# Attention scores of a hybrid decoder layer: both products of a score block over all 128 rows of the array

## The chip, the core and the metric

The kernel runs on one core of a Trainium2 chip. A core has a matrix engine (TensorE, in the profile PE for its matmuls and PEld for its weight loads), a vector engine (VectorE, DVE), a scalar engine (ScalarE, ACT), a general engine (GpSimd, POOL) and a queue that mostly issues transfers (SyncE, SP). Each works through its own list of instructions in order, and they wait for each other by semaphores. TensorE multiplies a stationary operand, which is loaded into its array of 128 by 128 cells first, with a moving operand that streams past it. The rows of the array are the dimension over which is summed; an operand that lies on only 64 of the 128 partitions of the on-chip memory uses only 64 rows. Products are added up in PSUM.

The metric is the device time of one execution in microseconds (us).

## What is computed

One hybrid decoder layer on 512 tokens of width 1024, in float32: a layer norm, a token mixer made of an SSD (state space) branch and an attention branch, and a SwiGLU feed-forward part, each added to its input and normalized again. Only the attention branch is touched by the change. It has 16 query heads of width 64, two key heads (eight query heads share one), blocks of 128 queries, and a window of 128 keys:

```
qb = (q * (hd ** -0.5)).reshape(bsz, nb, ATT_BLOCK, nkv, ng, hd)
...
k_band = jnp.concatenate([kb[:, :-1], kb[:, 1:]], axis=2)
v_band = jnp.concatenate([vb[:, :-1], vb[:, 1:]], axis=2)
scores = jnp.einsum('bnqkgd,bnskd->bnkgqs', qb, k_band).astype(jnp.float32)
...
scores = jnp.where(valid[None, :, None, None], scores + bias, -jnp.inf)
...
m = jnp.maximum(jnp.max(scores, axis=-1, keepdims=True), sink)
p = jnp.exp(scores - m)
p = p / (jnp.sum(p, axis=-1, keepdims=True) + jnp.exp(sink - m))
out = jnp.einsum('bnkgqs,bnskd->bnqkgd', p.astype(v.dtype), v_band)
```

## The kernel before

All large products run in a float32 form of reduced width that TensorE takes quickly (fp32r). To keep the precision, each operand is split into a high part and a rest, `hi` and `lo`, and a product is made of three matmuls, hi times hi, hi times lo and lo times hi (`mm3`, lines 146 to 150). The weights come in 164 units of 128 by 1024 numbers. ScalarE makes the `hi` of a unit (line 134) and VectorE the `lo` (line 135), up to three units ahead of their use.

TensorE's order is written out by hand. The input layer norm and the first products (key, value, first query tile, and dt for the SSD decays) come first, up to about 49 us. Then the attention runs in eight steps t of two heads each. Between its parts a `Filler` emits pieces of other products (k-tile steps of three matmuls on `ps_mm`: the next query tiles, the first SSD group's inputs, the attention's gate), in fixed amounts `F_ATT`, so that TensorE has work while the softmax of a step is made on other engines. After the attention come the rest of the gate and the attention's output projection, the SSD, the mixing product and the feed-forward part.

One round of that loop (lines 652 to 671) emits on TensorE: the scores of step t+1 for its first head (8 matmuls), filler, the scores for its second head (8 matmuls), filler, the transposes of the probabilities of step t (`ps_pt`, line 477) with a little filler between the heads, the largest piece of filler, and the products with the values (`ps_o`, line 490, 16 matmuls), filler again. The other three engines' orders are made by a scheduler from the same program.

`scores(t)` (line 412) makes, for each head j and each half of the four query blocks, a PSUM tile `ps_sc` with two blocks n. A query tile `q_f` (`q`) holds for head j the query's `hi` on the head's own 64 partitions and the query's `lo` on the other 64 (`evac_q`, lines 390 to 398). A key tile `kd` holds the key's `hi` in column block 0 and its `lo` in column block 1, each of them on both halves of the partitions (`evac_k`, lines 625 to 629). So the first matmul of a block (line 432) runs over 128 rows and gives (hi + lo) of the query times hi of the key; the second (line 434) takes only the 64 partitions of `js`, and adds the query's hi times the key's lo. VectorE then puts the window together (line 439, `copy_predicated`) and adds the distance penalty (line 441). From there the softmax goes on: the maximum (line 447), exponentials on ScalarE (line 459), the sum and its reciprocal (lines 461 and 462), the scaling on GpSimd (line 464). The transposed probabilities are taken out of PSUM by ScalarE (line 479), GpSimd (line 480) and VectorE (line 483) into `pT`.

The eight matmuls of one head in one step follow each other without anything between them. They are called a score stretch below; there are 16 of them, and each is followed by filler.

Of the kernel before, what the change touches and what calls it, by code (L numbers as in the profile page):

```python
# [18 lines left out]
P = 128  # L19
S = 512  # L20
D = 1024
NT = S // P            # token tiles = chunks = query blocks
KD = D // P            # k-tiles of the model width
NQ = 8                 # q feature tiles (two heads each)
NG = 4                 # SSD groups
NH = 32                # SSD heads
NF = 22                # FFN hidden tiles
# [3 lines left out]
LAST = 7               # k-tiles of the last product that finish one token tile after the other  # L31
RAW = 4                # weight units loaded ahead
# amounts of products (0.65 for a k-tile step) between the parts of the attention and SSD chains
# [4 lines left out]
# order of the weight units in the packed array; each unit is [128, 1024]  # L38
U_K, U_V, U_Q = 0, 1, 2
U_XBC = 10             # 24 tiles: xs 16, B 4, C 4  # L40
# [4 lines left out]
U_YA = 74              # per group 4 units of [4 k-tiles x 256 columns]  # L45
U_MIX = 90             # per k-tile
U_FG = 98
U_FU = 120
U_FD = 142             # per k-tile
N_UNITS = 164  # L50

# columns of the packed per-partition parameters
C_CW = 0               # 24 x 4
C_CB = 96              # 24
C_DS = 120             # 16
C_NW = 136             # 16
C_DTB = 152            # 1
C_LN = 153             # 3 layer norms x (gain 8, bias 8)
# [4 lines left out]
def kernel(  # L63
# [15 lines left out]
    PSUM = bass.MemoryType.PSUM  # L79
# [8 lines left out]
    # ---------------------------------------------------------------- constants  # L88
# [19 lines left out]
    # ---------------------------------------------------------------- weights  # L108
    class Units:
        """Loads and splits the weight units in the order of their use."""  # L110
# [27 lines left out]

        def next(self, unit, kt=KD, ahead=None):
            """hi, lo of the unit as [128, kt, 1024 / kt]."""  # L140
            assert self.order[self.pos] == unit, (self.pos, self.order[self.pos], unit)
            self.prepare(self.pos + (self.ahead if ahead is None else ahead))
            self.pos += 1
            return tuple(a.rearrange("p (k n) -> p k n", k=kt) for a in self.split.pop(self.pos - 1))
# [7 lines left out]
    class Filler:  # L152
        """Products in steps of one k-tile, emitted between the parts of the attention and SSD chains."""
# [30 lines left out]
    # ---------------------------------------------------------------- layer norm  # L184
    def ln_stats(pl, src, between=None, cuts=(0, 512, 1024)):
        """Mean and sqrt(var + eps) of each row of src [128, 1024]."""
        n = len(cuts) - 1
        st = pl.tile([P, 4, 6], F32, name="ln_st", tag="ln_st", bufs=2)[:, 0:n]
        for i in range(n):
            nc.vector.bn_stats(out=st[:, i], in_=src[:, cuts[i]:cuts[i + 1]])  # L190
            if i == 0 and between:
                between()
        mv = pl.tile([P, 2], F32, name="ln_mv", tag="ln_mv", bufs=3)
        nc.vector.bn_aggr(out=mv, in_=st)
        rs = pl.tile([P, 1], F32, name="ln_rs", tag="ln_rs", bufs=3)
        nc.scalar.activation(rs, mv[:, 1:2], AF.Sqrt, bias=eps_t, scale=1.0)
        return mv[:, 0:1], rs
# [5 lines left out]
    def affine(src, dst, gb):  # L203
        """Off the critical path: gain and bias on the token-major rows."""
        nc.gpsimd.tensor_mul(dst, src, gb[:, 0])
        nc.gpsimd.tensor_add(dst, dst, gb[:, 1])
# [4 lines left out]
    def transposed_k(pp, f, srcs, k, ln, hi, lo, lo_eng, on_act=False, between=None):  # L211
        """Normalized token tiles -> hi/lo of the layer norm's feature tile k, feature-major."""
        n = len(srcs) * P
# [22 lines left out]
    # the order of use of the weight units up to the gated sum  # L236
# [37 lines left out]
    def product(unit, a_hi, a_lo, evac):  # L274
        """Feature-major output tile of a unit of 8 k-tiles; evac takes it out of PSUM."""
        ps = acc_tile("ps_mm")
        hi, lo = units.next(unit)
        for k in range(KD):
            mm3(ps, (hi[:, k], lo[:, k]), (a_hi[:, k], a_lo[:, k]), k == 0, k == KD - 1)
            if k == KD - 1:  # L280
                evac(ps)
            yield

    # ---------------------------------------------------------------- dt and the decays
    # columns of the [128, 128] arrays: (g, j, c, t) for head 8 g + 2 t + j of chunk c
# [8 lines left out]
    def dt_chain(dtr, ps):  # L294
# [13 lines left out]
        # softplus(v) = max(v, 0) + log(1 + e), e = exp(-|v|);  # L308
        # log(1 + e) = 2 s (1 + s^2 / 3 + s^4 / 5 + ...), s = e / (2 + e)
# [13 lines left out]
        # dA = dt * -exp(a_log)  # L323
# [26 lines left out]
    # ---------------------------------------------------------------- conv + silu  # L350
    xbc_t = {}

    def g_xbc(g, i):
        """Feature tile i of group g's (B, C, xs0..3): projection, convolution along tokens, silu."""
# [22 lines left out]
    # ---------------------------------------------------------------- attention + its branch  # L377
# [7 lines left out]
    # hi and lo of each key head, on both halves of the partitions  # L385
# [4 lines left out]
    def evac_q(t, ps):  # L390
        """Head j's hi stays on its half of the partitions and lo goes to the other."""
# [20 lines left out]
    def scores(t):  # L412
        kv, q = t // 4, q_t[t]
# [5 lines left out]
        for j in range(2):  # L419
            js = slice(64 * j, 64 * j + 64)  # L420
            for half in range(2):
                # for each query block the key block before it and its own (the first has only its own)
                ps = axt([P, 2, 2, P], "ps_sc")
                for i in range(2):
# [3 lines left out]
                    def keys(a):  # L428
                        return a.unsqueeze(1).broadcast_to([a.shape[0], 2, P]) if n == 0 else a

                    # (hi + lo) k_hi over both halves of the partitions, then hi k_lo
# [3 lines left out]
                        ps[:, i], q[js, j, n * P:(n + 1) * P], keys(kd[kv][js, 1, ks]), start=False, stop=True)  # L435
                # the window has each key position of a block once: up to the query in its own block,
                # beyond it in the block before
# [33 lines left out]
    def weighted_values(t):  # L471
        kv, sc = t // 4, att_p.pop(t)
        pT = at.tile([P, 2, 7, P], F32, name="pT", tag="pT", bufs=1)
        for j in range(2):
# [3 lines left out]
            # blocks 2 n: keys of block n up to the query; 2 n + 1: those beyond it, for the next queries  # L478
# [28 lines left out]
    # distance of query and key: within the first block (out of reach beyond the query), then in the window  # L507
# [4 lines left out]
    def keep(a, past, fill):  # L512
        """Keeps the keys past the query, or those up to it."""
# [14 lines left out]
    # ---------------------------------------------------------------- input layer norm, first products  # L528
# [14 lines left out]
    def warm_up(n):  # L543
        """Keeps the tensor engine's clock up before the first products."""
        for _ in range(n):
            nc.tensor.transpose(ps_warm, ident, ident)
# [6 lines left out]
    with tc.manual_schedule(engines={mybir.EngineType.DVE, mybir.EngineType.Activation}):  # L553
        # the square root's table, before its first use
# [28 lines left out]
        def part(k, o, a, b):  # L583
            """One of a product's three passes: hi (0) or lo (1) of the weights with that of the input."""
# [3 lines left out]
        def part_dt(k, b):  # L588
            """hi and lo of the weights side by side, both with hi of the input, then hi with lo."""
# [4 lines left out]
        # the first parts in the order in which their operands come  # L594
# [81 lines left out]
    # what would have changed the activation table between the exponentials  # L676
# [8 lines left out]
    # ---------------------------------------------------------------- SSD  # L685
    # the attention's pool goes when its last users have been emitted, before the SSD's tiles
# [17 lines left out]
    def ssd_pre(i):  # L704
        """The decays within chunk c, and from its start."""
        g, c = divmod(i, NT)
        # L[s, (j t), l] = exp(acum[l] - acum[s]) for s <= l, else 0
# [21 lines left out]
    def ssd_a(i):  # L729
        """C B^T times the decays; token-major X dt, X dt decay and B."""  # L730
# [37 lines left out]
    def ssd_b(i):  # L768
        """Yields between the part within the chunk and the part of the state."""
# [44 lines left out]
    def gate_norm(g):  # L814
# [13 lines left out]
        # sums over the features, on every partition  # L828
# [17 lines left out]
    def g_ya(g, i, evac):  # L846
        """Two output tiles of group g's part of w_ssd_out."""
# [21 lines left out]
    def g_ga(f):  # L869
        def evac(ps):  # L870
            sga[f] = ph1.tile([P, S], F32, name="sga", tag="xs", bufs=8)
            nc.scalar.activation(sga[f], ps, AF.Sigmoid)
            # what the last group's product does not touch
# [61 lines left out]
    # ---------------------------------------------------------------- gated sum  # L935
# [17 lines left out]
    # ---------------------------------------------------------------- output projection, layer norm  # L953
    # of the output projection's units all but the first stay for the second half of the tokens
# [69 lines left out]
    # ---------------------------------------------------------------- FFN  # L1024
# [17 lines left out]
    # the first tiles by halves of the tokens, under the layer norm of the second half  # L1042
# [91 lines left out]
    # the last columns: what is there of them now, and the rest by halves in banks of their own  # L1134
# [21 lines left out]
def _layout(inp):  # L1156
    """Packs the inputs: weights as [unit, 128, 1024], vectors as columns of 128 partitions."""
# [3 lines left out]
    def tiles(w, k):  # L1161
        # [K, N] -> [N / n, 128, k, n] with k * n = 1024
# [54 lines left out]
```

## Time and profile before

| | us |
|---|---|
| median of 3 runs | 1075.58 |
| lowest and highest of them | 1075.5 and 1076.6 |
| span of the profiled execution, first to last instruction | 1074.2 |
| TensorE busy in that span | 1049.8 |
| VectorE busy | 613.3 |
| ScalarE busy | 465.2 |
| GpSimd busy | 245.4 |

The profile shows one execution. Its time is known as its span alone; the median of the runs is 1.4 us above it, which is about what lies around the first and last instruction. Each group of the profile names the line, engine and operation and the tiles it writes and reads; shapes such as `64*128 64x256` for a matmul are the rows and columns of the array in use and then what is written. Matmuls are pipelined, and the recorded length of one reaches past the start of the next, so what a matmul costs in a row of them is the distance from its start to the next one's start.

The attention's loop runs from about 56 us to 221 us. In that stretch TensorE has no recorded gap.

### The profile page before, as it was taken

To read this page: it belongs to the slowest core of one execution; us is meant where nothing else is said; L and a number is where in the kernel's file an instruction comes from. 1 tells how busy PE (TensorE), PEld (TensorE's weight loads), DVE (VectorE), ACT (ScalarE), POOL (GpSimd) and SP (SyncE) were. 2 spreads that over 40 slices of the span, in tenths; PEclk is the share of its full clock that TensorE was granted. 3 is DMA by queue.
4 is the path that set the end of the run, shared out by engine and by line. 5 is a ranking of instruction groups with operands and counts; after the bars stand their busy time and mean duration, and the time that the engine had idled before them with its cause. 6 is when DMAs were issued, how large, how long until landed. Compare 5 with 4: busy or idle time off the path is not lost.

```text
span 1074.2 us, 13041 instructions
## 1 busy us (share of the span) xinstructions
PE 1049.8 (98%) x5023; PEld 845.1 (79%) x5023; DVE 613.3 (57%) x834; ACT 465.2 (43%) x735; POOL 245.4 (23%) x219
## 2 busy tenths in 40 slices
PE   7899999999999899999999999999999999999997
PEld 6677777778788688788878878798888888888885
DVE  6967875433575874595575486664533333332665
ACT  4345445671545664564372443333433333332440
POOL 5601112100534532333340640164000000000000
PEclk9999999999999899999999999999999999999999
DMA  7312112123545233334333245314433333332471
GB/s 264 129 52 70 50 59 65 58 93 99 142 129 145 84 109 118 98 112 144 89 92 114 81 173 196 115 43 149 165 118 118 117 118 113 108 115 76 141 249 42
DMA packets 37502, 122.34 MB, mean 114 GB/s; under 512 B 4384, under 2 KB 4896, under 8 KB 37056
## 3 DMA queue, kind: packets, MB, share of 16 engines
q1 hardware_dynamic: 36224, 117.19, 33.4%
q10 hardware_dynamic: 576, 2.10, 0.6%
q0 software_dynamic: 640, 2.23, 0.5%
q8 instruction: 39, 0.64, 0.2%
q14 instruction: 23, 0.19, 0.1%
HBM read 117.17 MB, written 4.33 MB: 113 GB/s over the span
## 4 chain that ended last, share of the span: by engine, by line
PE 90%; DVE 4%; DMA 2%; POOL 1%; issue 1%; ACT 1%; SPq 0%; POOLq 0%; DVEq 0%; ACTq 0%
PE ps_mm L148 15%; PE ps_mm L149 14%; PE ps_mm L150 14%; PE ps_ff L148 8%; PE ps_ff L150 7%; PE ps_ff L149 7%; PE ps_da L148 2%; PE ps_da L149 2%; PE ps_da L150 2%; PE ps_sc L434 2%; PE ps_sc L432 2%; PE ps_yd L802 1%; PE ps_mix L148 1%; PE ps_mix L149 1%; PE ps_mix L150 1%; DVE w_lo L135 1%
## 5 line engine op out<-in xcount | busy, mean ns | idle before, releaser
L134 ACT CAST w_hi<-w_raw 128x1024 fp32r<-128x1024 f32 x185 | 193.4, 1050 | 337.2 <-PE ps_mm L149 129.2
L135 DVE TENSOR_TENSOR w_lo<-w_raw,w_hi 128x1024 fp32r<-128x1024 f32 x184 | 237.6, 1295 | 172.4 <-ACT w_hi L134 170.2
L148 PE MATMUL ps_mm<-hT_hi,w_hi 128*128 128x512 f32 x504 | 205.4, 408 | 0.4 <-DVE dtr L296 0.4
L149 PE MATMUL ps_mm<-hT_lo,w_hi 128*128 128x512 f32 x504 | 197.2, 391 | 0.0
L150 PE MATMUL ps_mm<-hT_hi,w_lo 128*128 128x512 f32 x504 | 197.2, 391 | 0.0
L148 PE MATMUL ps_ff<-h2T_hi,w_hi 128*128 128x512 f32 (+1 forms) x384 | 143.6, 374 | 0.0
L150 PE MATMUL ps_ff<-h2T_hi,w_lo 128*128 128x512 f32 (+1 forms) x384 | 142.9, 372 | 0.0
L149 PE MATMUL ps_ff<-h2T_lo,w_hi 128*128 128x512 f32 (+1 forms) x384 | 142.5, 371 | 0.0
L148 PEld LDWEIGHTS ps_mm<-hT_hi,w_hi 128*128 128x128 f32 x504 | 94.9, 188 | 24.8 <-issue 4.2
L150 PEld LDWEIGHTS ps_mm<-hT_hi,w_lo 128*128 128x128 f32 x504 | 94.9, 188 | 20.4
L149 PEld LDWEIGHTS ps_mm<-hT_lo,w_hi 128*128 128x128 f32 x504 | 95.1, 189 | 18.5 <-issue 1.0
L150 PEld LDWEIGHTS ps_ff<-h2T_hi,w_lo 128*128 128x128 f32 x384 | 72.3, 188 | 12.9
L149 PEld LDWEIGHTS ps_ff<-h2T_lo,w_hi 128*128 128x128 f32 x384 | 72.4, 188 | 12.8
L148 PEld LDWEIGHTS ps_ff<-h2T_hi,w_hi 128*128 128x128 f32 x384 | 72.3, 188 | 12.6
L721 POOL TENSOR_TENSOR L<-L,nac 128x512 f32<-128x512 f32 x32 | 42.2, 1337 | 95.7 <-DMA L<-a_d 88.6
L1066 DVE TENSOR_TENSOR sgf<-sgf,ps_ff 128x512 f32<-128x512 f32 x22 | 15.1, 686 | 68.7 <-PE ps_ff L150 68.7
L148 PE MATMUL ps_mm<-yh,w_hi 128*128 128x512 f32 x128 | 50.9, 398 | 0.0
L149 PE MATMUL ps_mm<-yl,w_hi 128*128 128x512 f32 x128 | 50.0, 391 | 0.6 <-DVE yl L230 0.6
L150 PE MATMUL ps_mm<-yh,w_lo 128*128 128x512 f32 x128 | 49.9, 390 | 0.0
L369 DVE SCALAR_TENSOR_TENSOR cacc<-ps_mm,pc,cacc 128x511 f32<-128x511 f32 (+2 forms) x54 | 40.1, 742 | 6.7 <-ACT cacc L366 6.0
L746 DVE TENSOR_TENSOR L<-L,cb 128x1024 f32<-128x1024 f32 x16 | 24.1, 1508 | 30.2 <-ACT cb L744 17.7
L763 POOL TENSOR_TENSOR Xd<-X,dec 128x256 f32<-128x256 f32 x24 | 18.1, 768 | 81.5 <-DVE X L752 81.5
(256 smaller groups left out, 1753.0 us busy)
## 6 DMA issues: line engine op xcount, KB each, us to landing
w_raw<-in_wall_dram SPq DMA_DIRECT2D x187, 512.0 KB, 3.5
L<-a_d SPq DMA_DIRECT2D x16, 512.0 KB, 5.2
E<-e_d SPq DMA_DIRECT2D x24, 128.0 KB, 3.1
h_d<-ln_t POOLq DMA_DIRECT2D x4, 512.0 KB, 3.2
h_r<-h_d ACTq DMA_DIRECT2D x4, 512.0 KB, 4.4
out_dram<-y_o SPq DMA_DIRECT2D x7, 256.0 KB, 4.1
x_sb<-in_x_dram SPq DMA_DIRECT2D x3, 512.0 KB, 7.1
ln_t<-in_ln_in_dram SPq DMA_DIRECT2D x1, 1024.0 KB, 9.5
```

The lines of the kernel that those rows point to most:

```text
L134: (copy or nc.scalar.copy)(out=hi, in_=w)
L135: self.last = (eng or nc.vector).tensor_sub(out=lo, in0=w, in1=hi.bitcast(F32))
L148: nc.tensor.matmul(ps, lh, rh, start=start, stop=False)
L149: nc.tensor.matmul(ps, lh, rl, start=False, stop=False)
L150: nc.tensor.matmul(ps, ll, rh, start=False, stop=stop)
L369: nc.vector.scalar_tensor_tensor(out=acc[:, d:], in0=ps[:, :S - d], scalar=pc[:, cw + 3 - d:cw + 4 - d], in1=acc[:, d:], op0=ALU.mult, op1 ...
L432: nc.tensor.matmul(ps[:, i], q[:, j, n * P:(n + 1) * P], keys(kd[kv][:, 0, ks]), start=True, stop=False)
L434: nc.tensor.matmul(ps[:, i], q[js, j, n * P:(n + 1) * P], keys(kd[kv][js, 1, ks]), start=False, stop=True)
L721: nc.gpsimd.tensor_tensor(out=L[:, j], in0=L[:, j], in1=nac5[:, g, j, c].unsqueeze(2).broadcast_to([P, 4, P]), op=ALU.add)
L746: nc.vector.tensor_tensor(out=Lf, in0=Lf, in1=cb.unsqueeze(1).broadcast_to([P, 8, P]), op=ALU.mult)
L763: nc.gpsimd.tensor_tensor(out=Xd[:, :, j], in0=X[:, :, j], in1=dec5[:, g, j, c].unsqueeze(2).broadcast_to([P, 4, 64]), op=ALU.mult)
L1066: nc.vector.tensor_mul(sg, sg, pu)
```

## The change

The second matmul of every score block takes all 128 partitions of the query and key tiles, as the first does, in place of the 64 of `js`, which goes. It then adds (hi + lo) of the query times lo of the key: the product of the two rests, which was left out before, is now in it. The number of matmuls, weight loads and other instructions stays, and so do their order on each of the five engines and their waits. Comments are taken out of the file too, and since one line goes, everything behind it stands one line higher in the profile of the changed kernel (434 becomes 433).

```diff
         for j in range(2):
-            js = slice(64 * j, 64 * j + 64)
             for half in range(2):
...
                     nc.tensor.matmul(
                         ps[:, i], q[:, j, n * P:(n + 1) * P], keys(kd[kv][:, 0, ks]), start=True, stop=False)
                     nc.tensor.matmul(
-                        ps[:, i], q[js, j, n * P:(n + 1) * P], keys(kd[kv][js, 1, ks]), start=False, stop=True)
+                        ps[:, i], q[:, j, n * P:(n + 1) * P], keys(kd[kv][:, 1, ks]), start=False, stop=True)
```

## The prediction

> **What bounds the kernel now.** I read the page first, then the chain of waits inside the attention, then the score matmuls by tile, then one score stretch in the order of time.
>
> ```profile
> span 1074.2 us, 13041 instructions
> ...
> PE 1049.8 (98%) x5023; PEld 845.1 (79%) x5023; DVE 613.3 (57%) x834; ACT 465.2 (43%) x735; POOL 245.4 (23%) x219
> ...
> PE 90%; DVE 4%; DMA 2%; POOL 1%; issue 1%; ACT 1%; SPq 0%; POOLq 0%; DVEq 0%; ACTq 0%
> ```
>
> TensorE is busy 98% of the span, and 90% of the chain that ended last lies on it. That is an average, so the attention has to be looked at by itself. The chain of waits between 50 and 220 us, by line:
>
> ```profile
> by line: PE ps_mm L148 23.7%; PE ps_mm L150 21.2%; PE ps_mm L149 21.0%; PE ps_sc L434 11.7%; PE ps_sc L432 10.0%; PE ps_o L490 7.4%; PE ps_pt L477 4.2%; PE ps_vt L639 0.3%; PE ps_dtT L303 0.2%; PE ps_tot L337 0.1%; PE ps_acT L339 0.1%; PE p
> ```
>
> Only TensorE stands in it, and the two score lines have 21.7% of 170 us, 36.9 us. So time saved on the score matmuls is on the path that sets the end, as long as no other engine comes up behind. The score matmuls by tile (durations are shortest, median and longest in ns):
>
> ```profile
> L432 PE MATMUL ps_sc<-kd,q_f x64: 279/383/388, 56.5 to 194.6; 128*128 128x256 f32 x64
> ...
> L434 PE MATMUL ps_sc<-kd,q_f x64: 378/382/384, 56.7 to 194.9; 64*128 64x256 f32 x64
> ```
>
> 128 matmuls, in 16 stretches of eight. The half-height ones are no shorter than the others: what they cost is not in the number of rows. One stretch in the order of time (start, length, both in us):
>
> ```profile
> 61.06 0.39 PE L148 MATMUL ps_mm<-hT_hi,w_hi 128*128 128x512 f32 x1
> 61.29 0.39 PE L149 MATMUL ps_mm<-hT_lo,w_hi 128*128 128x512 f32 x1
> ...
> 61.74 0.28 PE L432 MATMUL ps_sc<-kd,q_f 128*128 128x256 f32 x1
> 61.95 0.18 PEld L434 LDWEIGHTS ps_sc<-kd,q_f 64*128 64x128 f32 x1 [0.24 <-issue]
> 61.95 0.38 PE L434 MATMUL ps_sc<-kd,q_f 64*128 64x256 f32 x1
> 62.26 0.19 PEld L432 LDWEIGHTS ps_sc<-kd,q_f 128*128 128x128 f32 x1
> ...
> 64.14 0.50 PE L148 MATMUL ps_mm<-hT_hi,w_hi 128*128 128x512 f32 x1
> ...
> 64.47 0.39 PE L149 MATMUL ps_mm<-hT_lo,w_hi 128*128 128x512 f32 x1
> ```
>
> Each score matmul starts 0.31 us after the one before (61.95 to 62.26), and its weight load starts with it, not before it: at every change between 128 and 64 rows the next weights are loaded only when the array is through with the matmul before. The stretch takes 64.14 - 61.74 = 2.40 us. The filler matmul behind it is another such change: its successor starts 0.33 us later (64.14 to 64.47), against 0.23 us in plain filler (61.06 to 61.29).
>
> Now the same size of matmul with no change of rows, in the last product of the kernel, where each matmul also has weights of its own:
>
> ```profile
> 1061.27 0.28 PE L148 MATMUL ps_end<-w_hi,hB_hi 128*128 128x256 f32 x1
> 1061.27 0.19 PEld L149 LDWEIGHTS ps_end<-w_lo,hB_hi 128*128 128x128 f32 x1
> 1061.39 0.28 PE L149 MATMUL ps_end<-w_lo,hB_hi 128*128 128x256 f32 x1
> ...
> 1061.51 0.28 PE L150 MATMUL ps_end<-w_hi,hB_lo 128*128 128x256 f32 x1
> ```
>
> They start 0.12 us apart, and the load for the second starts with the first matmul, under it. The load alone is recorded as 0.19 us, longer than the distance, so loads and matmuls are pipelined there.
>
> **The change part by part.** It adds, removes and moves no instruction. The second matmul of a block goes from 64 to 128 rows, so the changes of rows between the two matmuls of a block and from one block to the next go, and with them the change back to the filler.
>
> *A score stretch.* Before: 2.40 us, and 0.33 us of the filler matmul behind it. After: 8 x 0.12 = 0.96 us, and 0.23 us. Saved: (2.40 + 0.33) - (0.96 + 0.23) = 1.54 us, and 16 x 1.54 = 24.6 us in all. The new price is borrowed from another product, since no row of before shows two 128-row score matmuls in sequence. From above it is bounded by today's 0.31 us (nothing saved). From below by matmuls of half as many columns:
>
> ```profile
> 80.20 0.71 PE L477 MATMUL ps_pt<-ident,sc 128*128 128x128 f32 x5
> ...
> L477 PE MATMUL ps_pt<-ident,sc 128*128 128x128 f32 x64 | 9.3, 273 | 0.0
> ```
>
> Five of them within 0.71 us, the last of which is recorded as 0.27 us, makes (0.71 - 0.27) / 4 = 0.11 us each; with that 16 x 8 x 0.01 = 1.3 us more would go. I take 0.12 us, of the row that has the same columns, rows and number type.
>
> The Trainium skill, "TensorEngine Tiling (Array Packing)", section "Key Properties", says that a change of the tiling mode drains the engine; the trace agrees, 0.31 us against 0.12 us. It gives no length for the drain, so the sum by it is the one above.
>
> *The other half of the keys' rests.* The second matmul now reads them, but they are written at the same place as before:
>
> ```profile
> 54.88 0.69 DVE L629 TENSOR_TENSOR kd<-ps_k,kd 64x512 fp32r<-64x512 f32 x1
> ```
>
> This is the last of four such writes, done at 55.57 us, and the first score matmul starts at 56.51 us in its order behind the filler. Its first matmul of 128 rows waits for VectorE already. The price is nothing; if that cover of 0.9 us went, the loss would be at most that, once.
>
> *Who comes up behind.* A round of the attention has two stretches and becomes 2 x 1.54 = 3.1 us shorter, while VectorE's work in it stays. Its busy time in four rounds, by windows that begin with a round's scores (length, then the busy time of PE, PEld, DVE, ACT and POOL with their instructions, the granted clock, the transfers' share and GB/s):
>
> ```profile
> 89.77:109.73 19.96, 19.96 (x97) 14.43 (x95) 15.46 (x34) 10.13 (x29) 4.65 (x6) 1.00 0.15 53
> 109.73:129.19 19.46, 19.46 (x92) 14.13 (x91) 15.47 (x46) 8.03 (x25) 1.83 (x3) 1.00 0.15 54
> 129.19:149.33 20.14, 20.14 (x98) 14.85 (x97) 15.57 (x31) 9.96 (x30) 5.44 (x8) 1.00 0.18 60
> 149.33:168.80 19.47, 19.47 (x93) 14.14 (x91) 13.48 (x25) 8.70 (x25) 3.27 (x4) 1.00 0.16 55
> ```
>
> The fullest, the second, would have 19.46 - 3.1 = 16.4 us for 15.47 us of work. What VectorE waits for in it:
>
> ```profile
> DVE pT L483 <- ACT pT L479: 1.8, 1, 1.8
> DVE sm L461 <- ACT sc L459: 1.0, 1, 1.0
> DVE q_f L396 <- ACT q_f L395: 0.5, 1, 0.5
> DVE xs_f L369 <- ACT xs_f L366: 0.4, 1, 0.4
> ```
>
> The first wait goes back to TensorE's transposes and shrinks when these come earlier. The other three, 1.9 us, may stay: 15.47 + 1.9 = 17.4 us, 1.0 us too much. Where that would be felt is `ps_o`, which waits for `pT`, the tightest joint that I found:
>
> ```profile
> 145.00 0.69 DVE L483 TENSOR_TENSOR pT<-ps_pt,tri 128x512 f32<-128x512 f32 x1
> ...
> 146.86 0.44 PE L490 MATMUL ps_o<-pT,v_sb 128*64 128x256 f32 x2
> ```
>
> It has 146.86 - 145.69 = 1.2 us to spare, in the round after the fullest. So 1.0 us of backlog would just be covered, and I put this term at nothing. It costs up to 3.1 us a round where the cover fails. The softmax that the transposes wait for has more room in the rounds, and least in the first:
>
> ```profile
> 74.26 2.03 POOL L464 TENSOR_TENSOR sc<-sc,sm 128x512 f32<-128x512 f32 x2 [26.47 <-DVE sm L462]
> ```
>
> It ends at 76.29 us, 3.9 us ahead of the transposes at 80.20 us; between that step's scores and these transposes lie the two stretches of the next step, so 3.1 of the 3.9 us go and 0.8 us remain.
>
> *Everything behind the attention* moves forward as a whole: weights are loaded as buffers come free, and no start is tied to a time. One thing is: the clock. At the one long wait of TensorE later on the granted clock halves for a while (same columns):
>
> ```profile
> 355.00:360.00 5.00, 1.85 (x9) 1.20 (x7) 2.67 (x4) 2.97 (x4) 4.92 (x4) 0.96 0.00 0
> 360.00:365.00 5.00, 4.17 (x20) 2.88 (x21) 2.82 (x3) 3.85 (x5) 1.33 (x3) 0.50 0.08 18
> 365.00:370.00 5.00, 5.00 (x20) 3.99 (x20) 4.80 (x5) 4.07 (x6) 0.00 (x0) 0.85 0.73 249
> ...
> 360.83 0.79 PE L831 MATMUL ps_ms<-sqr,ones_r 128*128 128x512 f32 x1 [3.97 <-ACT sqr L229]
> ```
>
> A wait of 3.97 us there costs 5 x 0.50 + 5 x 0.15 = 3.25 us of clock behind it. How much of that falls on matmuls may come out otherwise once the wait lies elsewhere; I keep 3.25 us to both sides for the range.
>
> Sum: the profiled execution goes from 1074.2 to 1074.2 - 24.6 = 1049.6 us; the median of the runs lies 1.4 us above the span (1075.58), so 1051.0 us.
>
> **The rivals.**
>
> A, **VectorE becomes the bound** in the three rounds from 89.77 to 149.33 us, which have over 15.4 us of its work because the SSD's decays are made there too. If they keep their length, 3 x 3.1 = 9.3 us come back: 1060.3 us. For it speaks the 1.0 us too much above; against it that the two other rounds have room (16.9 and 17.0 us for 15.5 and 15.6 us), and that VectorE's waits for score matmuls shrink.
>
> B, **the change does nothing**: score matmuls of 128 rows stay 0.31 us apart, because two matmuls in the same rows can't have the second's load under the first. Then 1075.6 us. Against it stands `ps_end`, where the load starts with the matmul of the same rows ahead of it; for it only that no row shows the score operands so. The Trainium skill, "TensorE: Matmul & The Clock Gate", section "The mechanism", has this very rule, that loads overlap with running matmuls only where the row groups differ. The `ps_end` rows contradict it, 0.12 us apart on the same rows.
>
> C, **slower**: the waits of A grow long enough to lower the clock. Place: `ps_o` behind `pT`. Price: 4.0 us of wait and 3.25 us of clock behind it, as at 360 us, 7.2 us a round. It decides from four rounds on: 4 x 7.2 - 24.6 = 4.2 us, 1079.8 us. Against it: a wait of 4 us needs a round of 20.4 us, and VectorE has 15.57 us of work in the fullest.
>
> **How the numbers follow.** Forecast 1051.0 us, chance 0.80; A 0.13; B 0.05; C 0.02. The forecast's own range is 1051.0 - 1.3 - 3.25 = 1046.5 up to 1054.3 us. To leave out no more than 2 in 10 it is taken to 1057 us, where two of A's three rounds give back all they won (1051.0 + 6.2). 0.2% is 2.2 us, about what a measurement of this kernel can tell from no change. Faster: forecast and A, 0.93; within it: B, 0.05; slower: C, 0.02.
>
> **What would show it.** In the changed kernel's trace a score stretch should take 0.96 us, its matmuls start 0.12 us apart at about 0.28 us each, with the weight load one matmul ahead, and the filler behind it should go on after 0.23 us. The rounds should be 16.4 to 17.0 us, with the value products not waiting for `pT`. A would show as gaps ahead of `ps_o` or `ps_pt` while VectorE has none, B as unchanged distances. I am wrong if the distances fall and the time does not: then a wait that I called covered is not.

## The result and the profile after

The changed kernel takes 1050.04 us (median of 4 runs, 1049.24 to 1050.64) against 1076.09 us of the kernel before beside it: a ratio of 0.976, with a 95% interval of 0.9749 to 0.9772. That is 26.1 us less. The profiled execution's span went from 1074.2 to 1047.5 us, 26.7 us less.

The page of the changed kernel, the same three lines:

```profile
span 1047.5 us, 13041 instructions
...
PE 1023.7 (98%) x5023; PEld 836.4 (80%) x5023; DVE 612.1 (58%) x834; ACT 464.9 (44%) x735; POOL 246.5 (24%) x219
...
PE 89%; DVE 4%; DMA 2%; issue 2%; POOL 2%; ACT 1%; SPq 0%; POOLq 0%; DVEq 0%; ACTq 0%
```

The same instructions ran, TensorE's busy time fell by 26.1 us, the other engines' hardly at all, and TensorE still bounds the whole. The score matmuls by tile in the changed kernel:

```profile
L431 PE MATMUL ps_sc<-kd,q_f x64: 279/279/280, 56.2 to 169.3; 128*128 128x256 f32 x64
...
L433 PE MATMUL ps_sc<-kd,q_f x64: 277/279/284, 56.3 to 169.5; 128*128 128x256 f32 x64
```

Both forms have 128 rows now, and both are recorded at 0.28 us, where 0.38 us stood before. The second score stretch in the order of time, the one that the prediction shows of before:

```profile
59.89 0.28 PE L431 MATMUL ps_sc<-kd,q_f 128*128 128x256 f32 x1
59.89 0.19 PEld L433 LDWEIGHTS ps_sc<-kd,q_f 128*128 128x128 f32 x1
60.01 0.28 PE L433 MATMUL ps_sc<-kd,q_f 128*128 128x256 f32 x1
...
60.72 0.19 PEld L148 LDWEIGHTS ps_mm<-hT_hi,w_hi 128*128 128x128 f32 x1
60.83 0.39 PE L148 MATMUL ps_mm<-hT_hi,w_hi 128*128 128x512 f32 x1
...
61.05 0.39 PE L149 MATMUL ps_mm<-hT_lo,w_hi 128*128 128x512 f32 x1
```

Each load now starts with the matmul ahead of its own (59.89), and the filler's load does so too (60.72, ahead of 60.83). The stretch takes 60.83 - 59.89 = 0.94 us instead of 2.40 us, and the filler goes on after 0.22 us instead of 0.33 us.

Where the 26.7 us come from can be read at landmarks that both traces have. The last round's value products, before and after:

```profile
218.98 0.44 PE L490 MATMUL ps_o<-pT,v_sb 128*64 128x256 f32 x2
```

```profile
193.17 0.44 PE L489 MATMUL ps_o<-pT,v_sb 128*64 128x256 f32 x2
```

They start 25.8 us earlier. 0.3 us of that stood already at the first score matmul (56.5 and 56.2 us), which the change can't have caused; 25.5 us fall into the attention. The remaining 0.9 us arise behind it: 1.6 us are won at the long wait in the SSD, and 0.7 us are lost again further back. That wait in the changed kernel, and the stretches around it:

```profile
333.50:338.50 5.00, 4.05 (x21) 2.69 (x22) 2.81 (x3) 3.75 (x5) 1.43 (x3) 0.66 0.07 11
338.50:343.50 5.00, 5.00 (x24) 4.12 (x23) 4.70 (x5) 4.08 (x5) 0.00 (x0) 1.00 0.74 257
...
334.43 1.52 PE L830 MATMUL ps_ms<-sqr,ones_r 128*128 128x512 f32 x2 [3.40 <-ACT sqr L229]
```

The wait is 3.40 us instead of 3.97 us, and the clock lost is 5 x 0.34 = 1.7 us instead of 3.25 us. In the starts of TensorE's matmuls 0.6 us of the gain lie at the wait, and 1.0 us behind it, since in the kernel of before the clock fell 1.2 us ahead of the wait's end (at 359.6 us), so that a part of its low time cost nothing.

VectorE in the three fullest rounds, windows that begin with a round's scores (columns as in the prediction), and the joint that is the tightest now (the value products of the round from 99.92 us):

```profile
83.16:99.92 16.76, 16.76 (x97) 13.51 (x96) 15.71 (x34) 10.13 (x29) 4.64 (x6) 1.00 0.19 64
99.92:116.18 16.26, 16.26 (x92) 13.21 (x91) 14.93 (x45) 7.05 (x24) 1.04 (x2) 1.00 0.15 46
116.18:133.12 16.94, 16.94 (x98) 13.94 (x97) 15.96 (x32) 10.91 (x31) 6.22 (x8) 1.00 0.27 90
...
112.45 0.69 DVE L482 TENSOR_TENSOR pT<-ps_pt,tri 128x512 f32<-128x512 f32 x1
...
113.71 0.65 PE L489 MATMUL ps_o<-pT,v_sb 128*64 128x256 f32 x4
```

Each of these rounds is 3.2 us shorter, TensorE has no gap in any of them, and VectorE fills up to 94% of one. At `ps_o` 113.71 - 113.14 = 0.6 us are left. The joint that the prediction shows, one round further on, still has 1.2 us.

### The profile page after: what moved, and what is told of

The parts are those of the page before. It is cut to its first block, busy times and chain, and to the rows that moved or that the text cites. A ratio compares the mean times of both kernels' runs of the same rounds, so it can differ in the third digit from the quotient of the medians.

```text
span 1047.5 us, 13041 instructions
## 1 busy us (share of the span) xinstructions
PE 1023.7 (98%) x5023; PEld 836.4 (80%) x5023; DVE 612.1 (58%) x834; ACT 464.9 (44%) x735; POOL 246.5 (24%) x219
## 4 chain that ended last, share of the span: by engine, by line
PE 89%; DVE 4%; DMA 2%; issue 2%; POOL 2%; ACT 1%; SPq 0%; POOLq 0%; DVEq 0%; ACTq 0%
PE ps_mm L148 14%; PE ps_mm L149 14%; PE ps_mm L150 14%; PE ps_ff L148 8%; PE ps_ff L150 8%; PE ps_ff L149 8%; PE ps_da L148 2%; PE ps_da L149 2%; PE ps_da L150 2%; PE ps_db L149 1%; PE ps_mix L149 1%; PE ps_mix L148 1%; PE ps_mix L150 1%; PE ps_db L150 1%; PE ps_db L148 1%
## 5 line engine op out<-in xcount | busy, mean ns | idle before, releaser
L134 ACT CAST w_hi<-w_raw 128x1024 fp32r<-128x1024 f32 x185 | 193.4, 1050 | 321.7 <-PE ps_ff L149 125.4
L148 PE MATMUL ps_mm<-hT_hi,w_hi 128*128 128x512 f32 x504 | 203.1, 403 | 0.7 <-DVE dtr L296 0.7
```

Source lines behind the costliest of these rows:

```text
L134: (copy or nc.scalar.copy)(out=hi, in_=w)
L148: nc.tensor.matmul(ps, lh, rh, start=start, stop=False)
```

## The experiments

Two questions stood. Is the cost that went a price of each change between 128 and 64 rows (theory D), or of a 64-row matmul as such (rival H)? And how far is VectorE from becoming the bound? All times are medians, and each ratio is to runs of the kernel before on the same chip; the changed kernel was not run again beside the experiments, so they are compared with it by their ratios.

**Both matmuls over 64 rows.**

```diff
-  ps[:, i], q[:, j, n * P:(n + 1) * P], keys(kd[kv][:, 0, ks]), start=True, stop=False)
+  ps[:, i], q[js, j, n * P:(n + 1) * P], keys(kd[kv][js, 0, ks]), start=True, stop=False)
```

> Kernel of before, but the first matmul of every score block takes only the 64 partitions of its head too (it leaves out the query's lo times the key's hi). No change of rows is left inside a score stretch, two are left per stretch (from the filler and back to it). Theory D, the cost is paid at each change between 128 and 64 rows: the eight changes of a stretch of before cost (2.40 + 0.33) - (0.94 + 0.23) = 1.56 us, 0.195 us each; six of them go, so score matmuls start 0.12 us apart and the time falls by 16 x 6 x 0.195 = 18.7 us, to about 1057 us. Rival H, a matmul over 64 rows costs 0.31 us by itself, whatever stands ahead of it: distances stay 0.31 us, time 1076 us or a little more.

Measured: 1057.0 us, ratio 0.9817 (0.9801 to 0.9833), 19.4 us less than before. Rows of a stretch in its trace:

```profile
59.60 0.39 PE L150 MATMUL ps_mm<-hT_hi,w_lo 128*128 128x512 f32 x1
59.92 0.18 PEld L432 LDWEIGHTS ps_sc<-kd,q_f 64*128 64x128 f32 x1 [0.35 <-issue]
59.92 0.38 PE L432 MATMUL ps_sc<-kd,q_f 64*128 64x256 f32 x1
60.03 0.19 PEld L434 LDWEIGHTS ps_sc<-kd,q_f 64*128 64x128 f32 x1
...
60.71 0.18 PEld L434 LDWEIGHTS ps_sc<-kd,q_f 64*128 64x128 f32 x1
60.82 0.27 PE L434 MATMUL ps_sc<-kd,q_f 64*128 64x256 f32 x1
61.03 0.50 PE L148 MATMUL ps_mm<-hT_hi,w_hi 128*128 128x512 f32 x1
```

Inside the stretch matmuls of 64 rows start 0.11 us apart, as fast as those of 128 rows (0.12 us), with their loads one ahead (the last load, at 60.71 us, stands 0.11 us ahead of its matmul at 60.82 us). At both ends the change shows: the first load waits until the filler is through (59.60 to 59.92, 0.32 us instead of 0.23 us), and so does the filler's behind it (60.82 to 61.03, 0.21 us instead of 0.12 us). Rival H falls.

**The same matmuls, fewer changes.** The kernel of before with its 64 matmuls of 128 and 64 of 64 rows, in another order within a stretch:

```diff
+  # 128, 128, 64, 64, 64, 64, 128, 128 rows
+  for i in range(2):
+      for lo in (i, 1 - i):
+          for half in range(2):
+              block(half, i, lo, lo == i)
```

> Kernel of before, with the same 128 score matmuls (64 of them over 64 rows) in another order within a stretch: 128, 128, 64, 64, 64, 64, 128, 128 rows, so that two changes of rows are left per stretch in place of eight. Theory D (cost per change, 0.195 us): six of eight go, 16 x 6 x 0.195 = 18.7 us less, about 1057 us. Rival H (each 64-row matmul costs its 0.39 us more than a 128-row one in a row, with its neighbours): their number stays, so about 1076 us.

Measured: 1057.38 us, ratio 0.9815 (0.9799 to 0.9831). Its second stretch:

```profile
60.61 1.48 PE L428 MATMUL ps_sc<-kd,q_f 128*128 128x256 f32 x8
61.81 0.19 PEld L148 LDWEIGHTS ps_mm<-hT_hi,w_hi 128*128 128x128 f32 x1
61.92 0.39 PE L148 MATMUL ps_mm<-hT_hi,w_hi 128*128 128x512 f32 x1
...
62.15 0.39 PE L149 MATMUL ps_mm<-hT_lo,w_hi 128*128 128x512 f32 x1
```

The eight matmuls (merged into one row; half of them have 64 rows) take 61.92 - 60.61 = 1.31 us, and the filler goes on after 0.23 us. With two changes at 0.195 us on top of 0.94 us it should be 1.33 us. The same products are computed as before (in half of the blocks the two are added up in the other order), and 19.0 us of 26 are there. So it is the number of changes that counts, and theory D holds in size.

**More work for VectorE in every round,** by doing the maximum three times over, in the changed kernel and in that of before:

```diff
+  nc.vector.tensor_reduce(out=nm, in_=sc, op=ALU.max, axis=AX.X, negate=True)
+  nc.vector.tensor_reduce(out=nm, in_=sc, op=ALU.max, axis=AX.X, negate=True)
   nc.vector.tensor_reduce(out=nm, in_=sc, op=ALU.max, axis=AX.X, negate=True)
```

> Changed kernel with the reduction of the maximum made three times over in each of the eight rounds, two more of 1.21 us, 2.4 us of VectorE work a round. Theory V, VectorE is close behind TensorE in the changed kernel: room in the rounds from 83.16, 99.92, 116.18 and 133.12 us is length less VectorE's busy time less its waits for ScalarE, 16.76-15.71-1.0, 16.26-14.93-1.0, 16.94-15.96-0.7, 16.27-13.19-2.0, that is 0.05, 0.33, 0.28 and 1.1 us; 2.4 us overshoot it by 2.4, 2.1, 2.1 and 1.3 us, 7.9 us in all, less the 0.6 us that the value products have to spare: time about 1057 us, with gaps ahead of the transposes or the value products. Rival F, TensorE alone sets the length: 1050 us.

> Kernel of before with the same two extra reductions a round. Theory V: room in the three fullest rounds is 19.96-15.46-1.0 = 3.5, 19.46-15.47-1.9 = 2.1 and 20.14-15.57-0.8 = 3.8 us, so 2.4 us are hidden but for 0.3 us at most: 1076 us. Rival F: 1076 us too; if this kernel gets longer by several us, the extra reductions cost by themselves (on the softmax's chain) and not for want of room, and the run of the changed kernel with them says nothing on room.

Measured: 1058.91 us (ratio 0.9832, 0.9818 to 0.9847) and 1081.7 us (1.0054, 1.0039 to 1.0069). The changed kernel came out close to V's number, but the kernel of before lost 5.3 us as well, so by what was written down ahead this pair says nothing on room. The trace of the padded changed kernel shows where most of it was lost, in the first round:

```profile
75.86 0.66 PE L478 MATMUL ps_pt<-ident,sc 128*128 128x128 f32 x4 [1.69 <-POOL sc L465]
77.84 1.11 PE L478 MATMUL ps_pt<-ident,sc 128*128 128x128 f32 x4 [1.33 <-POOL sc L465]
...
77.00:83.80 6.80, 5.96 (x16) 4.88 (x17) 5.83 (x10) 3.14 (x11) 1.78 (x3) 0.50 0.25 77
```

The transposes wait 3.0 us there for the softmax of their step, since the extra reductions lie on that chain and the scheduler set VectorE's order anew around them. From 77.0 us on the granted clock stands at 0.50 for 6.8 us, which costs up to 3.4 us more. This round is 6.2 us longer than without the reductions, and in the kernel of before it is 4.4 us longer. So this part comes from the length of the chain and from the clock behind the waits. Three later rounds of the changed kernel lose 2.9 us, and two of that of before 1.8 us; there the value products wait for VectorE's `pT`.

**More work off the chain.** The penalty tiles `bp` are written again and again in three steps; nothing waits for the extra writes but what stands behind them on VectorE.

```diff
   for j in range(2):
-      nc.vector.tensor_scalar_mul(bp[:, j], relm, -(2.0 ** (-0.5 * (2 * t + j + 1))))
+      for _ in range(6 if 2 <= t <= 4 else 1):
+          nc.vector.tensor_scalar_mul(bp[:, j], relm, -(2.0 ** (-0.5 * (2 * t + j + 1))))
```

> Changed kernel; the penalty tiles bp (line 417, off the softmax's chain) of the steps 2, 3 and 4 are written six times over, ten more writes of about 0.2 us, 2.0 us of VectorE work in each of the three fullest rounds. Theory V (VectorE is close behind TensorE there): room is 0.05, 0.33 and 0.28 us, and 1.0, 1.0 and 0.7 us more where the writes fall into its waits for ScalarE; 2.0 us overshoot it by 1.0, 0.7 and 1.0 us, less 0.6 us to spare: about 2 us longer, 1052 us. Rival L, what stands close behind TensorE is the length of the first round's softmax chain alone, and work in the later rounds is free: 1050 us.

> Kernel of before with the same extra writes. Theory V: room with the waits for ScalarE is 4.5, 4.0 and 4.6 us a round, so 2.0 us are hidden: 1076 us. Rival L: 1076 us too.

Measured: 1051.88 us (0.977, 0.9752 to 0.9788) and 1076.42 us (1.0002, 0.9992 to 1.0011). The first ratio's interval overlaps that of the changed kernel without the writes, so the time does not decide between V and L. That it is V's number is chance: of the 1.7 us by which the profiled execution is longer, 0.4 us stood already at the first score matmul and 0.9 us arose behind the attention. The trace says more. VectorE in two of the three fullest rounds:

```profile
83.55:100.30 16.75, 16.75 (x96) 13.51 (x95) 16.56 (x40) 10.13 (x29) 5.08 (x6) 1.00 0.18 64
100.30:116.84 16.54, 16.54 (x93) 13.65 (x92) 16.29 (x47) 6.63 (x23) 1.04 (x2) 1.00 0.12 37
...
113.57 0.69 DVE L483 TENSOR_TENSOR pT<-ps_pt,tri 128x512 f32<-128x512 f32 x1
...
114.10 2.00 PE L490 MATMUL ps_o<-pT,v_sb 128*64 128x256 f32 x16
```

The writes did not fall where the expectation put them. Ten of the 30 extra ones stand in these two rounds, five in each, about 2.0 us in both together; the other 20 were made in the lighter rounds ahead. VectorE is busy for 0.85 and 1.36 us more than without them, 16.56 + 16.29 = 32.85 of 33.29 us, and the two rounds together are only 0.27 us longer (16.76 and 16.26 us without the writes). That is lost at a joint of the kind named in the prediction: `pT` is ready at 114.26 us, after `ps_o` has started. So VectorE's waits for ScalarE could be filled almost to the end: 2.2 us of work found room where V, with these waits, counts 1.05 + 1.33 = 2.38 us.

**Twice as much,** eleven times over in the steps 3, 4 and 5 (`range(11 if 3 <= t <= 5 else 1)`):

> Changed kernel; the penalty tiles of the steps 3, 4 and 5 are written eleven times over, twenty more writes of about 0.2 us, 4 us of VectorE work in each of three rounds, 12 us in all. Theory V2 (VectorE's whole idle time in those rounds can be filled, its waits for ScalarE too, and no more): idle in the rounds from 83.16, 99.92 and 116.18 us is 1.05, 1.33 and 0.98 us, 3.1 us more in the lighter round behind them and 0.6 us to spare at the value products, about 7 us in all; 12 - 7 = 5 us come out, 1055 us, with TensorE waiting at the value products or transposes. Rival L (only the softmax chain's length stands behind TensorE): about 1050 to 1051 us.

> Kernel of before with the same writes. Theory V2: idle in its three rounds from 89.77, 109.73 and 129.19 us is 4.5, 4.0 and 4.6 us, 13 us for 12 us of work: 1076 us, at most 1 or 2 us more. Rival L: 1076 us. The difference between this kernel and the changed one with the same writes shrinks from 26 to about 21 us by V2, and stays at 26 us by L.

Measured: 1055.48 us (0.9807, 0.9791 to 0.9824) and 1076.45 us (1.0006, 0.9996 to 1.0016). The same work costs no time that can be told from noise before (its trace has one wait of 0.9 us, at `ps_pt`), and about 5 us in the changed kernel, 0.9807 against 0.976. The waits of TensorE between 50 and 200 us in its trace (none are recorded there without the writes), the round in which they lie, and the clock behind them:

```profile
PE ps_tot L337 <- DVE sc L441: 1.4, 1, 1.4
PE ps_acT L339 <- DVE sc L441: 0.6, 1, 0.6
...
115.57:136.69 21.12, 19.13 (x98) 15.11 (x97) 20.92 (x53) 11.53 (x31) 6.45 (x8) 0.92 0.22 78
...
125.60:129.00 3.40, 3.40 (x11) 2.43 (x10) 3.27 (x10) 1.92 (x7) 1.04 (x2) 0.50 0.02 5
```

The waits are not at `ps_pt` or `ps_o`, as V2 had it, but at small products of the SSD decays that stand between, waiting for a VectorE that is behind. All that is lost in the attention is lost in this one round: it takes 21.12 us instead of 16.94 us, 4.2 us more, and VectorE is busy for 20.92 us of it. 2.0 us of that are the waits, and the clock at 0.50 for 3.4 us makes up to 1.7 us more; the run does not tell apart what VectorE's backlog and the clock cost together. Only a third of the extra writes, about 4 us, stand in this round; the other two of the fullest rounds, ahead of it, are as long as without the writes. So V2's sum of 5 us came out, but not by its count: it has the writes spread over three rounds, and it has no clock in it. L, which had 1050 to 1051 us, falls.

## Why the prediction was right

*TensorE bounds the attention.* Right: 25.5 us of the matmuls' time came out of the attention as time, and TensorE has no recorded wait there.

*A score stretch.* Measured were 0.94 us and 0.22 us behind it, (2.40 + 0.33) - (0.94 + 0.22) = 1.57 us, 25.1 us in 16 stretches, where the forecast had 1.54 and 24.6 us. The price borrowed from `ps_end` was right to 2%. The runs with both matmuls over 64 rows and with two changes per stretch show that what it rested on, a price per change of rows, is the cause: six of eight changes gone gave 19.4 and 19.0 us where 18.7 us were due.

*Rival B*, that two matmuls in the same rows can't overlap with loads, is refuted by the stretch above, and also, by the run with both matmuls over 64 rows, for two 64-row matmuls in the same 64 rows. Read by itself, the rule that the Trainium skill states in "TensorE: Matmul & The Clock Gate", section "The mechanism", does not hold for the forms of this kernel: loads start with the matmul ahead of their own in the same rows, 0.12 and 0.11 us apart.

*Who comes up behind.* The term was put at nothing and is nothing. The counting behind it was too strict, though: it gave 1.0 us too much work for the fullest round. In the trace that round has 14.93 us of work and 1.0 us of waits for its 16.26 us: 0.5 us of the work moved to its neighbours (46.60 us in the three rounds, 46.50 us before), and of the 1.9 us of waits that were kept as fixed 0.9 us went. The extra writes show that the rest of these waits can be filled too. What is left of rival A is its direction: the same extra work costs about 5 us now and nothing that can be told from noise before, so VectorE is the next bound. How much work away it is over the whole attention stays open, since the writes bunched in one round and the clock fell there too.

*The rest moves as a whole.* Right but for the wait in the SSD and the clock behind it, within the 3.25 us that the range allowed for. The span fell by 26.7 us instead of 24.6 us. Of the 2.1 us between, 0.3 us lie ahead of the attention, 0.9 us in it (0.5 us in the score stretches) and 0.9 us behind it. The median shows only 1.0 us of them, since the profiled execution was the shortest of the four: its span lies 2.5 us below the median, and the sum carried over 1.4 us. Why the low clock lasted less long was not tried, and it need not come from the change: the run with both matmuls over 64 rows waits 3.6 us at the same place and has the clock at 0.50 for 6.8 us, the changed kernel with the extra writes of steps 2 to 4 waits 4.1 us and has it for 3.4 us.

*Rival C* did not occur; the granted clock stood at 1.00 in all rounds. But it counted only with waits of 4.0 us, as at 360 us. In the run with writes eleven times over the clock fell to 0.50 behind two waits of 1.4 and 0.6 us.

## What to carry to other kernels

In this kernel a matmul over half of the array's rows is hardly cheaper than one over all of them (0.11 and 0.12 us from start to start), and where the two kinds alternate each change costs about 0.195 us; at each of them the next weights are no longer loaded under the running matmul. Fill the unused rows with something that adds a harmless term or zero, or put matmuls of one kind together. To find such places, look in the order of time for weight loads that start together with their own matmul instead of the one before.

## What the runs showed that I had not expected

The remaining matmuls over half of the array's columns have the same gap. In the changed kernel the filler ahead of the last value products, and these, with 64 columns (`128*64`):

```profile
192.85 0.39 PE L150 MATMUL ps_mm<-hT_hi,w_lo 128*128 128x512 f32 x1
193.17 0.44 PE L489 MATMUL ps_o<-pT,v_sb 128*64 128x256 f32 x2
```

0.32 us lie between the starts instead of 0.23 us, as at a change of rows. Whether full-width value products would be worth it was not tried.
